# Most tiles of a decoder layer's input projection as seven-product pairs, on one pool of slots

## The chip, the cores and the metric

The kernel runs on one core of a Trainium2 chip. The metric is the device time of one execution in microseconds, the median of several runs. The engines are called by the profile's names: PE is TensorE (PEld its weight loads), DVE is VectorE, ACT is ScalarE, POOL is GpSimd, SP is SyncE, which here only issues transfers.

## The reference

One inference step of one decoder layer, float32, for a prompt of 1024 tokens and 8 samples of 4 new tokens; the kernel treats them as one matrix of T = 1056 columns.

```
h = rmsnorm(x, ln1)
aq, ak, av, sh, sB, sC, dqkv, dz, da, db, gl = split(h @ w_in)     # 1024 x 7432
oa = sliding_window_attention(aq, ak, av, sinks)                   # window 128, 8 query heads, 2 kv heads
ob = sB * causal_dwconv(sC * sh, sc_conv_w)                        # width 3
oc = gated_deltanet(silu(causal_dwconv(dqkv)), dz, da, db)         # width 4, chunked, 4 heads
merged = gate0 * (oa @ w_br_a) + gate1 * (ob @ w_br_b) + gate2 * (oc @ w_br_c)   # gates = sigmoid(gl)
x = x + merged @ w_o
gate, val = split(causal_dwconv(rmsnorm(x, ln2) @ ffn_up, ffn_conv_w))
x = x + (silu(gate) * val) @ ffn_down                              # 2816 wide
y = rmsnorm(x, ln_f)
```

The conv, attention and delta states of both groups are outputs too.

## The kernel before, in words

**Products.** Data lies with channels on the 128 partitions and the 1056 columns behind one another. Each float32 operand is split into a high part (a cast on ACT) and a low part (the rest, on POOL or DVE, `split`, L215 to L218), and each product is three: high by high, high by low, low by high. A *single tile* (`job`, `proj`, `products`, L327) is 128 output channels: three groups of 352 columns, 8 blocks of input channels, three products each, 72 in all. Its weights (512 KB) come through two buffers `wr` on SP's queue, up to three tiles ahead, and are split whole into `wh` and `wl`.

A *pair* (`class Pairs`, L1408) computes two tiles in seven block products instead of eight, in Strassen's way. The weights and h are cut into 2 by 2 blocks; the seven pieces of the weights are made in `produce`, `ahead` pieces before their use (four need a sum of 512 columns, L1365 to L1371, all a split); the seven pieces of h (`b11`, `t1`, `t2`, `b22`, `t3`, `b21`, `t4`) are built once. Each piece is 24 products of 264 columns, 168 for a pair; partial results are copied out of PSUM (L1417) or added in passing (L1195 to L1197, L1436). The pair's 1 MB of weights comes on ACT's queue; with `single` there is one pair of `wr` buffers, so that a load waits until the pair before has split its last piece, else every other pair's weights go to slots and are loaded a pair ahead.

**Stages.** The first stage multiplies h by w_in (58 tiles). ORDER fixes its jobs; capitals are pairs, `G10` being tiles 0 and 1 of the second branch's gates. Then come twelve pairs that merge the branches (`mg`), eight single tiles of w_o (`wo_job`), 22 up pairs, and the down projection, whose weight sums are formed ahead by `weight_sums` and kept in DRAM.

Four D pairs of the delta net's q, k, v use h's pieces in the first stage. The pieces lie partly in place of h's own parts: t4 overwrites the second half of `hh` and `hl` for four of eight blocks. After the last D pair `last_d` reads those halves back from `hn_d` and splits them again, since single tiles follow; for the last three pairs, G22 to G26, `h_build` makes the pieces anew from `hh + hl` (L1777, L1791, L1800).

**Background.** The elementwise and small matrix work of the branches runs as generators ("lanes", class `Lanes`). Every few products the foreground calls `bg.tick`, which lets one lane that is ready do its next step; `now` is an estimate of the time from these ticks, and waits for transfers or for other engines are estimates too. What a lane issues goes into the same engine queues as the foreground's work, in program order for PE. `bg.until` ticks, with no foreground between, until a condition holds. Lanes that need PSUM banks for a while ask `banks(n)`, of 4 (of 2 during D pairs).

The delta net is `norm_lane`, `pass1` (8 chunks of 128 tokens, three lanes), `solve` (the inverse of 32 by 32 triangles on DVE), `merge` (larger blocks of the inverse), `prep` and `scan` (the recurrence), `sample_delta` for the samples, then `out_norm`. Attention is `sample_attn`, then `attn_blocks` (loads a block of keys and queries) and three lanes `units` (two units to a block, 16 in all, the result stored behind L1644). `load_operand` builds the seven pieces of a branch's output for the merge; the merge takes the branches in the order 1, 0, 2.

**Slots.** Nearly all SBUF is two pools of 4336-byte rows: `col` with 24 slots (foreground) and `sb` with 21 (background). `room(n)` and `room2(n)` hold a lane back until n are free; `lend` and `space` let attention use part of `col`.

Of the kernel before, what the change touches and what calls it, by code (L numbers as in the profile page):

```python
# [15 lines left out]
KD = 8  # L16
# [16 lines left out]
N_COL, N_BG = 24, 21  # L33
# [88 lines left out]
class Arena:  # L122


    def __init__(self, pool, tag, n):
        self.pool, self.tag, self.n, self.live = pool, tag, n, 0
# [20 lines left out]
    def room(self, n):  # L147
        return lambda: self.live + n <= self.n
# [3 lines left out]
RESERVE = 4  # L152
# [15 lines left out]
GVWAIT = 5.0  # L168
# [4 lines left out]
def trunk(tc, A, O, cst_d):  # L173
# [17 lines left out]
    col = Arena(cp, "col", N_COL)  # L191
    sb = Arena(cp, "bg", N_BG)
# [52 lines left out]
    hn_d = [dtile(f"hn_d{m}", [128, HT]) for m in range(4)]  # L245
# [7 lines left out]
    sfcw = cp.tile([128, 836], F32, name="sfcw")  # L253
# [163 lines left out]
    hh = [col.take([128, T], F32R) for _ in range(KD)]  # L417
    hl = [col.take([128, T], F32R) for _ in range(KD)]
# [3 lines left out]
    xt = [sb.take([128, D]) for _ in range(2)] + [col.take([128, D]) for _ in range(7)]  # L422
# [29 lines left out]
    def x_group(tg):  # L452
# [32 lines left out]
        if tg == NTG - 1:  # L485
            nc.scalar.copy(ones_r, ones_f)
            nc.scalar.copy(hot[:, 46:47], ones_f[:, 0:1])
            sb.drop(7)
            col.drop(7)
# [111 lines left out]
    def sums(src, sa, r, acc, wait):  # L601


        (hi, ha), (lo, la) = grab([128, T], F32R, sb), grab([128, T], F32R, sb)
# [85 lines left out]
    def d_start(room):  # L690
        bg.until(room)
        cb, ca = grab([128, 3 + SEQ + 56], first=col)
# [3 lines left out]
    def d_end(j, cb, ca):  # L696
# [6 lines left out]
        cv, sa = grab([128, 3 + SEQ + 56], first=col)  # L703
# [10 lines left out]
    def dqkv_job(j, first=False):  # L714
        def fn(wh, wl):
            cb, ca = d_start(col.room(1))
# [54 lines left out]
    def pass1(c):  # L771

        yield lambda: done.get("qkv", 0) == 12 and done.get("ab") and sb.live + 4 <= N_BG
        kq = sb.take([128, 8, 128]).rearrange("p (h s) t -> p h s t", s=2)
        kn, bcb = pair()
        gcb, Dt = pair()
        At, qk = pair()
# [35 lines left out]
        sb.drop(4)  # L813
        bump("p1")

    def solve():

        yield lambda: done.get("p1", 0) == NB and sb.live + 4 <= N_BG
        B, X, U, tm = (sb.take([128, 32, 32]) for _ in range(4))
# [18 lines left out]
        sb.drop(4)  # L838
        bump("solve")

    def merge():


        yield lambda: done.get("p1", 0) == NB and sb.live + 7 <= N_BG
        A, Ub, W64 = ([sb.take([128, 8, 128]) for _ in range(2)] for _ in range(3))
        xw = pair2()
        X11, W = xw
        for t in W64 + A + Ub:
            nc.gpsimd.memset(t, 0.0)
        zero = W64[0].rearrange("p a b -> p (a b)")  # L850
        for b in range(2):
            dma(u_d[:, 64 * b + 32:64 * b + 64, 64 * b:64 * b + 32].rearrange("q j i -> j q i"),
                zero[0:32].rearrange("p (q i) -> p q i", i=32))
            dma(u_d[16 * b:16 * b + 16, 64:128, 0:64].rearrange("q j i -> j q i"),
                zero[0:64].rearrange("p (q i) -> p q i", i=64))
# [6 lines left out]
        yield lambda: done.get("solve") and sb.live + 5 <= N_BG  # L862
        X21, U12 = pair2()
        A64 = [sb.take([128, 8, 128]) for _ in range(2)]
        X64, U64 = sb.take([128, 16, 64]), sb.take([128, 16, 64])
# [4 lines left out]
        there = bg.arrived()  # L870
        for t in A64 + [X64, U64]:
            nc.gpsimd.memset(t, 0.0)
        for hh in range(2):
            r = slice(64 * hh, 64 * hh + 64)
            for i in range(2):
                dma(A64[i][r, :, r], a64_d[:, eight(hh, i), :])
# [1577 lines left out]
```

## Time and profile before

| | us |
|---|---|
| median of 3 runs | 1914.05 (1909.06 to 1915.11) |
| the profiled execution | 1920.69 |
| its span, first to last instruction | 1918.9 |
| PE busy | 1795.1 (94%) |
| DVE, POOL, ACT busy | 1214.4, 1044.9, 811.2 |
| first single tile's first product | 15.4 |
| D pairs | 122.7 to 222.2 |
| last gate pair ends, merge begins | 944.9 |
| merge ends, w_o begins | 1096.4 |
| up stage | 1195.7 to 1651.5 |

The times of the jobs were found by counting products on the timeline: 72 of L327 to a tile, 168 (84 in the merge) of L1408 to a pair. The page's mean duration of a matmul is longer than its share of the time, since matmuls overlap; the pace is read from stretches that hold a known number of them.

### The profile page before, as it was taken

The numbers are of one execution on the slowest core, as the hardware profiler recorded it, in microseconds if no ns is written. First come the engines' busy times: TensorE is split into PE (matmuls) and PEld (weight loads), VectorE is DVE, ScalarE is ACT, GpSimd is POOL, SyncE is SP. The second block draws the span as 40 slices with busy tenths as digits, with TensorE's granted clock in tenths as the row PEclk, the third lists the DMA queues.
The fourth block names the chain that finished last, engine by engine and source line by source line (L and its number), as shares of the span: only waits on it lengthen the run. The fifth ranks groups of instructions, "written<-read, shape, count | busy, mean of one in ns | idle before, by whom it ended". The sixth has DMA issues, their size and how long they took to land. (4 is left out here: it accounts for less than half of the span.)

```text
span 1918.9 us, 33893 instructions
## 1 busy us (share of the span) xinstructions
PE 1795.1 (94%) x12862; PEld 1753.7 (91%) x12862; DVE 1214.4 (63%) x2102; ACT 811.2 (42%) x1738; POOL 1044.9 (54%) x973
## 2 busy tenths in 40 slices
PE   6899799989999999988988899999999999899997
PEld 5798799989999998978988899999999999899996
DVE  5678755641324566686699956777777777743344
ACT  5544621112124455434554445554554544444443
POOL 3656456422334345485467745876867777334442
PEclk8999999989899999999999999999999999999998
DMA  7212597457467675944463343233232232675652
GB/s 254 87 52 85 171 325 214 129 138 210 146 201 224 207 228 162 313 166 162 156 206 99 117 140 124 72 115 110 85 111 85 94 113 80 236 243 185 186 171 89
DMA packets 298452, 301.92 MB, mean 157 GB/s; under 512 B 56549, under 2 KB 229073, under 8 KB 298273
## 3 DMA queue, kind: packets, MB, share of 16 engines
q1 hardware_dynamic: 245136, 269.34, 43.7%
q10 hardware_dynamic: 53152, 30.41, 5.5%
q8 instruction: 101, 1.65, 0.4%
q14 instruction: 63, 0.51, 0.1%
HBM read 205.33 MB, written 96.36 MB: 157 GB/s over the span
## 5 line engine op out<-in xcount | busy, mean ns | idle before, releaser
L327 PE MATMUL mm<-col,wh 128*128 128x352 f32 x2472 | 626.2, 332 | 19.5 <-ACT col L1189 9.2
L327 PEld LDWEIGHTS mm<-col,wh 128*128 128x128 f32 x2472 | 443.4, 194 | 26.2 <-ACT col L1189 9.8
L327 PE MATMUL mm<-col,wl 128*128 128x352 f32 x1248 | 413.4, 331 | 0.5 <-DVE wl L218 0.5
L327 PEld LDWEIGHTS mm<-col,wl 128*128 128x128 f32 x1248 | 241.6, 194 | 1.8 <-DVE wl L218 0.7
L218 POOL TENSOR_TENSOR wl<-wr,wh 128x1024 fp32r<-128x1024 f32 x50 | 127.9, 2559 | 191.0 <-ACT wh L217 189.1
L218 POOL TENSOR_TENSOR wl<-col,wl 128x512 fp32r<-128x512 f32 (+1 forms) x90 | 114.5, 1273 | 104.2 <-ACT wl L217 96.0
L218 POOL TENSOR_TENSOR wh<-col,wh 128x512 fp32r<-128x512 f32 (+1 forms) x82 | 101.5, 1238 | 88.0 <-ACT wh L217 68.6
L217 ACT CAST wh<-wr 128x1024 fp32r<-128x1024 f32 (+2 forms) x96 | 77.2, 810 | 126.5 <-PE mm L327 72.9
L218 DVE TENSOR_TENSOR col<-col 128x528 fp32r<-128x528 f32 x72 | 59.6, 836 | 111.3 <-ACT col L217 100.8
L1408 PE MATMUL mm<-bg,wh 128*128 128x264 f32 x762 | 116.3, 290 | 10.8 <-DVE wh L218 4.0
L1408 PE MATMUL mm<-bg,wl 128*128 128x264 f32 x744 | 114.0, 290 | 8.2 <-ACT bg L1865 4.2
L1408 PEld LDWEIGHTS mm<-bg,wh 128*128 128x128 f32 x762 | 103.0, 193 | 12.6 <-DVE wh L218 4.2
L1408 PEld LDWEIGHTS mm<-bg,wl 128*128 128x128 f32 x744 | 101.0, 193 | 9.9 <-ACT bg L1865 4.5
L1408 PE MATMUL mm<-col,wh 128*128 128x264 f32 x630 | 101.9, 289 | 5.0 <-ACT col L1417 4.0
L217 ACT CAST col<-col 128x528 fp32r<-128x528 f32 (+1 forms) x114 | 70.2, 627 | 78.0 <-POOL wh L218 31.8
L217 ACT CAST wl<-col 128x512 fp32r<-128x512 f32 (+1 forms) x104 | 59.5, 573 | 94.4 <-PE bgps L1408 32.7
L1436 DVE TENSOR_TENSOR bgps<-bgps,col 128x264 f32<-128x264 f32 x136 | 58.5, 435 | 63.2 <-PE bgps L1408 62.6
L1408 PE MATMUL mm<-col,wl 128*128 128x264 f32 x552 | 91.0, 287 | 6.0 <-DVE bgps L1436 2.5
L1408 PEld LDWEIGHTS mm<-col,wh 128*128 128x128 f32 x630 | 87.9, 192 | 6.2 <-ACT col L1417 4.5
L2171 DVE SCALAR_TENSOR_TENSOR bgps<-col,sfcw,bgps 128x358 f32<-128x358 f32 (+1 forms) x168 | 89.4, 590 | 1.1 <-ACT bgps L2169 0.3
L1408 PE MATMUL bgps<-col,wl 128*128 128x264 f32 x498 | 81.5, 293 | 3.7 <-POOL wl L218 3.3
L217 ACT CAST wh<-col 128x512 fp32r<-128x512 f32 (+1 forms) x94 | 53.0, 565 | 72.3 <-PE bgps L1408 25.6
(546 smaller groups left out, 4747.7 us busy)
## 6 DMA issues: line engine op xcount, KB each, us to landing
wr<-in_w_in SPq DMA_DIRECT2D x44, 512.0 KB
g_d<-col SPq DMA_DIRECT2D x24, 528.0 KB
ht_d<-col SPq DMA_DIRECT2D x44, 264.0 KB
col<-ht_d SPq DMA_DIRECT2D x44, 264.0 KB
bg<-in_ffn_down SPq DMA_DIRECT2D x22, 512.0 KB
wr<-in_ffn_up ACTq DMA_DIRECT2D x22, 512.0 KB
col<-in_ffn_up ACTq DMA_DIRECT2D x22, 512.0 KB
col<-g_d SPq DMA_DIRECT2D x20, 528.0 KB
```

Source lines behind the costliest of these rows:

```text
L217: nc.scalar.copy(hi, src)
L218: eng.tensor_tensor(lo, src, f32(hi), op=ALU.subtract)
L327: mm(ps[:, :TG], a[:, k, :], b[k][:, cc], start=n == 0, stop=n == last)
L1408: mm(ps, w[:, x + k, :], b[y][:, c0:c0 + HU], start=not n and piece not in NESTED, stop=n == last, skip_group_check=piece in NESTED)
L1436: nc.vector.tensor_tensor(dst, ps, x, op=ALU.add)
L2171: nc.vector.scalar_tensor_tensor(ps, cb[:, a + i:b + i], w(i), ps, op0=ALU.mult, op1=ALU.add)
```

## The change

- 19 more pairs: of the first stage's 58 tiles only d4 to d7, q0 and q1 stay single. One object `hp` runs all 26 pairs with `single` weights; for pairs from the fifth on, no low part and two instead of four sums are made on DVE, the rest on POOL. The background's limit is 2 PSUM banks in all of them.
- h's pieces are built once and stay (12 slots beside h's own 16). `last_d`, `hn_d`, the second `h_build` are gone.
- Convolution, z, k and v, q tiles get pair versions (`sc_pair`, `z_pair`, `kv_pair`, `whole_pair`). `sc_pair` multiplies in place.
- One pool of 46 slots; `kept` holds some back from the background for `own`.
- Delta net: `pass1` takes 3 slots for 4, `solve` 3 for 4; `merge` starts when `solve` is done, and loads its second half's blocks after the first half; `prep` takes 3 for 4 and starts with the scan; `sample_delta` starts beside `solve`, with two state buffers for four, and reads two of the states twice.
- Attention starts when scan and `sample_delta` are both done; blocks take 4 free slots, at most two blocks ahead; units take 2 slots for 3.
- Branch order 1, 2, 0: branch 2 waits for `out_norm`, branch 0 for attention. Branch 1's operand is built inside the last pairs.
- `weight_sums` runs in the up stage, in place, with a wait after each pass. The conv weights of the last stage get a slot at the merge.

```diff
-N_COL, N_BG = 24, 21
+N_SLOT = 46
...
-AHEADB = 3
-GAHEAD, GADD, GLO = 3, (1, 2, 3, 4), (0, 2, 4, 6)
+AHEADB = 2
...
-DPAHEAD, DPADD, DPLO, DTICK = 3, (1, 2, 3, 4), (0,), 6
+HAHEAD, HADD, HLO, DTICK, HTICK = 3, ((1, 2, 3, 4), (1, 2)), ((0,), ()), 6, 4
+KEPT = 3
...
-d4 hbd q0 d5 d6 dpairs d7 D0 D2 D8 D10 delta
-sc_start c0 h0 c1 b0 h1 c2 b1 h2 c3 b2 h3 sc_end
-v b3 k q1 q2 q3 attn_in attn sums z0 z1 z2 z3
-g10 g11 g12 g13 g14 g15 g16 g17
-g00 g01 g02 g03 g04 g05 g06 hb g07 g20 pairs g21 G22 op1 G24 G26
+d4 hb q0 d5 q1 d6 pairs d7 D0 D2 D8 D10 delta
+C0 H0 B0 C2 H2 sc_end B2
+KV Q2 attn_in attn Z0 Z2 less
+G10 G12 G14 G16 G00 G02 G04 G06 G20 G22 op1 G24 G26
...
     def solve():
-        yield lambda: done.get("p1", 0) == NB and sb.live + 4 <= N_BG
-        B, X, U, tm = (sb.take([128, 32, 32]) for _ in range(4))
+        yield lambda: done.get("p1", 0) == NB and sb.room(3)()
+        B, X, tm = (sb.take([128, 32, 32]) for _ in range(3))
+        U = B
...
     def merge():
-        yield lambda: done.get("p1", 0) == NB and sb.live + 7 <= N_BG
+        yield lambda: done.get("solve") and sb.room(6)()
...
         sb.drop(5)
-        yield
+        yield sb.room(6)
+        A64, W64 = ([sb.take([128, 8, 128]) for _ in range(2)] for _ in range(2))
+        X64, U64 = sb.take([128, 16, 64]), sb.take([128, 16, 64])
+        for t in A64 + [X64, U64] + W64:
+            nc.gpsimd.memset(t, 0.0)
...
     def sample_delta():
-        yield lambda: done.get("merge") and sb.live + 4 <= N_BG and col.live + 7 <= N_COL
+        yield lambda: done.get("p1", 0) == NB and sb.room(6)()
...
     def attn_consts():
-        yield lambda: done.get("v") and done.get("attn_in") and sb.live + 2 <= N_BG
+        yield lambda: done.get("v") and done.get("attn_in") and done.get("o", 0) == 2 and sb.room(2)()
...
-            yield lambda: done.get("satt") and done.get("o") and nb - done.get("blk", 0) < AHEADB and space() >= 7
+            yield lambda: done.get("satt") and done.get("o", 0) == 2 and nb - done.get("blk", 0) < AHEADB and sb.room(4)()
...
-            yield lambda: nb in blocks and space() >= 3
+            yield lambda: nb in blocks and sb.room(2)()
...
+    def own(shape):
+        bg.until(room2(1))
+        sb.kept -= 1
+        return sb.take(shape)
...
-            limit[0] = 2 if pp is dpp else 4
-            pp.run(i, hb, out, after)
+            limit[0] = 2
+            hp.run(i, hb, out, after)
             limit[0] = 4
...
-    order = [(b, m) for b in (1, 0, 2) for m in range(0, 8, 2)]
+    ready = {0: lambda: done.get("att", 0) == 2 * NB + 1, 2: lambda: done.get("oc", 0) == 4}
+    order = [(b, m) for b in (1, 2, 0) for m in range(0, 8, 2)]
...
     def weight_sums():
...
-            tt(s1, a21, a22, op=ALU.add)
-            tt(s2, s1, a11, op=ALU.subtract)
-            yield
+            tt(a22, a21, a22, op=ALU.add)
+            yield bg.after(SUMWAIT)
...
     def up_phase():
         ffn_start()
+        bg.add(weight_sums())
```

## Rows read from the trace of the kernel before

**Rows 1.** The page's first lines: span; engine, busy us (share of the span) xinstructions.
```profile
span 1918.9 us, 33893 instructions
...
PE 1795.1 (94%) x12862; PEld 1753.7 (91%) x12862; DVE 1214.4 (63%) x2102; ACT 811.2 (42%) x1738; POOL 1044.9 (54%) x973
```

**Rows 2.** Stretches: us, busy us of PE, PEld, DVE, ACT, POOL, PEclk, DMA, GB/s.
```profile
122.70:222.20 99.50, 88.83 (x689) 85.67 (x688) 79.68 (x87) 51.22 (x91) 59.00 (x60) 0.98 0.27 86
222.20:251.80 29.60, 21.23 (x99) 19.86 (x98) 22.95 (x16) 12.92 (x23) 15.99 (x9) 0.71 0.96 333
251.80:814.70 562.90, 547.36 (x3499) 530.82 (x3498) 269.93 (x507) 167.44 (x385) 231.65 (x176) 0.97 0.69 204
814.70:904.00 89.30, 74.56 (x472) 72.95 (x471) 72.12 (x63) 35.09 (x71) 65.20 (x33) 0.90 0.49 166
904.00:944.90 40.90, 40.90 (x339) 40.90 (x338) 23.08 (x35) 19.89 (x43) 14.34 (x12) 1.00 0.32 113
944.90:1096.40 151.50, 131.59 (x977) 126.71 (x976) 143.45 (x264) 75.73 (x199) 104.74 (x96) 0.94 0.46 155
1223.10:1651.50 428.40, 428.40 (x3530) 427.82 (x3528) 325.87 (x694) 214.26 (x500) 308.12 (x384) 1.00 0.29 94
```

**Rows 3.** Stretches, PE only: length, busy us (xproducts), granted clock, DMA share, GB/s.
```profile
358.90:404.90 46.00, 46.00 (x291) 1.00 0.32 89
231.20:248.30 17.10, 12.74 (x45) 0.50 0.96 368
```

**Rows 4.** Timeline of PE: start, us, line, tiles, [idle before <- releaser].
```profile
231.86 1.34 PE L1408 MATMUL mm<-bg,wl 128*128 128x264 f32 x4 [4.18 <-ACT bg L1865]
...
868.33 0.96 PE L327 MATMUL mm<-col,wh 128*128 128x352 f32 x2 [8.33 <-ACT col L1189]
```

**Rows 5.** Groups, 122.7 to 222.2: count, busy us, mean ns, idle before.
```profile
L218 POOL TENSOR_TENSOR wh<-bg,wh 128x512 fp32r<-128x512 f32 x8 | 14.8, 1846 | 3.7 <-ACT wh L217 2.3 <-issue 1.3
...
L613 PE MATMUL bgps<-bg,hot 128*48 128x352 f32 x36 | 7.9, 328 | 5.0 <-DVE bg L218 3.2 <-ACT bg L217 1.8
...
L217 ACT CAST wh<-bg 128x512 fp32r<-128x512 f32 x8 | 5.0, 622 | 15.7 <-DVE bg L1371 6.5 <-DVE bg L1365 5.6 <-DVE bg L1369 1.5
```

**Rows 6.** Timeline around the load of the second D pair's weights.
```profile
142.86 0.38 ACTq L182 DMA_DIRECT2D wr<-in_w_in  x1
...
147.25 0.70 DVE L1365 TENSOR_TENSOR bg<-wr 128x512 f32<-128x512 f32 x1 [1.89 <-DMA wr<-in_w_in]
```

**Rows 7.** Groups of POOL, 251.8 to 404.9.
```profile
L218 POOL TENSOR_TENSOR wl<-wr,wh 128x1024 fp32r<-128x1024 f32 x12 | 29.2, 2430 | 23.8 <-ACT wh L217 23.8
```

**Rows 8.** The same stretch, POOL only: length, busy us, granted clock, DMA share, GB/s.
```profile
251.80:404.90 153.10, 75.85 (x66) 1.00 0.66 189
```

**Rows 9.** Groups of POOL, 222.2 to 944.9.
```profile
L218 POOL TENSOR_TENSOR wl<-wr,wh 128x1024 fp32r<-128x1024 f32 x38 | 97.2, 2558 | 153.5 <-ACT wh L217 151.6 <-PE mm L327 1.8
...
L1777 POOL TENSOR_TENSOR bg<-col 128x1056 f32<-128x1056 f32 x4 | 14.4, 3592 | 0.0
```

**Rows 10.** Waits of PE, 404.9 to 581.8: us in total, times, longest.
```profile
PE bgps L885 <- DMA bg<-xu_d: 6.3, 1, 6.3
```

**Rows 11.** Single lines: count, ns min/median/max, first to last start.
```profile
L796 PE MATMUL bgps<-bg x64: 377/379/381, 287.9 to 346.6; 128*128 128x256 f32 x64
...
L932 ACT COPY bg<-bgps x2: 585/586/586, 445.6 to 447.4; 128x512 f32<-128x512 f32 x2
...
L1014 ACT COPY bg<-bgps x3: 585/585/591, 513.1 to 550.5; 128x512 f32<-128x512 f32 x3
...
L1673 POOL COPY bg<-bg x2: 283/288/292, 521.6 to 524.5; 64x128 f32<-64x128 f32 x2
...
L1732 ACT COPY bg<-bgps x16: 163/167/169, 576.1 to 578.8; 64x16 f32<-64x16 f32 x16
...
L1644 DVE TENSOR_TENSOR col<-bgps,col x7: 669/681/683, 619.7 to 845.5; 64x512 f32<-64x512 f32 x7
```

**Rows 12.** Groups of POOL, 1223.1 to 1651.5.
```profile
L218 POOL TENSOR_TENSOR wl<-col,wl 128x512 fp32r<-128x512 f32 x41 | 54.7, 1334 | 38.9 <-ACT wl L217 37.1 <-PE bgps L1408 1.8
```

More of the change, by code (lines that the diff above doesn't have):

```diff
@@ L869, in merge @@
                 dma(Ub[i][r, :, r], xu_d[1][2 * b + 1, eight(hh, i)].rearrange("q i j -> i q j"))
[L870 to L876, printed above, removed]
-        for b, hh, r, gs in four:
-            d = slice(64 * hh + 32 * b, 64 * hh + 32 * b + 32), slice(32 * b, 32 * b + 32)
-            dma(X64[d[0], :, d[1]], xu_d[0][b, gs].rearrange("q i j -> i q j"))
-            dma(U64[d[0], :, d[1]], xu_d[1][2 + b, gs].rearrange("q i j -> i q j"))
-        yield there
+        yield bg.arrived()
         yield banks(1)
@@ L948, in prep @@
         for c in range(NB):
-            yield lambda: done.get("merge") and len(pre) < 2 and sb.live + 4 <= N_BG
+            yield lambda: done.get("scan") and len(pre) < 2 and sb.room(3)()
             kn, vT = pair()
             qT, ebc = pair()
-            qk, ke = pair()
-            vb, U = pair()
+            qk, U = pair()
+            ke, vb = vT, ebc
             dma(kn, qkv_d[c][:, 4:8, :])
@@ L1251, in sc_job, with times @@
-    def sc_job(kind, t):
-        c0, fn = {"c": (C_SC, sc_c), "h": (C_SH, sc_h), "b": (C_SB, sc_b)}[kind]
-        job(w_cols(w_in, c0 + t * 128), KD, fn(t))
-    named["sc_start"], named["sc_end"] = lambda: step(sc_start), lambda: step(sc_end)
-    for t in range(4):
-        for kind in "chb":
-            named[f"{kind}{t}"] = lambda kind=kind, t=t: sc_job(kind, t)
+    def times(dst, ps, x, part, view=lambda ap: ap):
+        y = ps[:, part]
+        if x is not None:
+            y = x[:, part]
+            nc.vector.tensor_tensor(y, ps[:, part], y, op=ALU.add)
+        nc.vector.tensor_tensor(dst, dst, view(y), op=ALU.mult)
@@ L1437, in summed, with stored, whole_pair, out @@
         return dst
[L1440 to L1451 removed]
+    def stored(dst_d, evac_of):
         def fn(wh, wl):
[L1453 to L1454 removed]
+            bg.until(room2(1))
+            t, ta = grab([128, T])
             proj(wh, wl, hh, hl, KD, evac_of(t))
[L1456 to L1462 removed]
+            dma(dst_d, t)
+            ta.drop()
+        return fn
+    def whole_pair(then, func=AF.Copy, scale=1.0):
+        ts = []
+        for _ in range(2):
+            ts.append(own([128, T]))
+        def out(which, c0, ps, x, more):
+            d = ts[which][:, c0:c0 + HU]
+            if x is None:
+                nc.scalar.activation(d, ps, func, scale=scale)
+            else:
+                nc.vector.tensor_tensor(d, ps, x, op=ALU.add)
+        def finish(which):
+            t = ts[which]
+            if func != AF.Copy or scale != 1.0:
+                cc = slice(which * HT, T)
+                nc.scalar.activation(t[:, cc], t[:, cc], func, scale=scale)
+            then(which, t)
+        return out, finish
     def token_major(src, blks, out):
@@ L1636, in units @@
             n, last = 0, 2 * len(kbs) - 1
-            for kb in kbs:
-                for b in (PTh, PTl):
-                    mm(ps, (vz if kb else vp)[:, kv, :], b[:, kb, :], start=n == 0, stop=n == last)
+            for kb, t in zip(kbs, pt):
+                for b in range(2):
+                    mm(ps, (vz if kb else vp)[:, kv, :], t[:, b, :], start=n == 0, stop=n == last)
                     n += 1
@@ L1886, in fn @@
                 last_sums()
-                for j in range(2, pp.ahead):
-                    pp.produce(j)
-                if not pp.single:
-                    pp.load(1)
-            end = i + 1 == len(pp.srcs)
+                for j in range(2, hp.ahead):
+                    hp.produce(j)
+            end = i + 1 == len(hp.srcs)
             out, finish = start()
+            hp.tick = DTICK if i < 4 else HTICK
             def after(j, piece):
@@ L2051, in weight_sums @@
         for p in range(NPAIR):
-            yield sb.room(3)
-            wa, wb, s = (sb.take([128, 1024]) for _ in range(3))
+            yield room2(4)
+            wa, wb = (sb.take([128, 1024]) for _ in range(2))
             for i, w in enumerate((wa, wb)):
```

493 lines of the change are left out of this document (228 added, 265 removed).

## The prediction

> **What bounds the kernel now.** I read the page's first part, then a table of stretches, then the waits of those in which TensorE is not full. TensorE is busy 1795.1 of 1918.9 us [rows 1]; columns removed from it count where it is full, elsewhere the wait counts. The table [rows 2] cuts out four pairs (122.7 to 222.2), one tile, c0 (to 251.8), 34 tiles beside delta net and attention (to 814.7), four tiles and the first gate pair (to 904.0), two gate pairs (to 944.9, TensorE full), the merge (to 1096.4), and 21 of the 22 up pairs from 1223.1, full throughout. Units: four undisturbed tiles take 46.0 us [rows 3], 11.50 each (72 products of 352 columns); 21 pairs take 428.4 [rows 2], 20.40 each (168 of 264 columns). A pair replaces two tiles, so it gives 23.00 - 20.40 = 2.60 us.
>
> A wait costs more than its gap: from 231.2, around the 4.18 us gap that ends at 231.9 [rows 4], the granted clock is 0.50 for 17.1 us [rows 3], the lower of its two levels (1.2 of 2.4 GHz).
>
> **The change part by part**, against the profiled execution's own 1920.69 us (1918.9 of span, 1.8 around it).
>
> *a. Nineteen more pairs.* 38 of the 44 single tiles of w_in become pairs: 12 gated-convolution tiles, v and k, two q, four z, 18 gate tiles. 19 x 2.60 = 49.4 us, all on TensorE's path. That q1 moves ahead of D0 changes no sum.
>
> *b. The restoring and rebuilding of h's pieces go.* Before, D10 ends with h's lost half read back and split again, and c0 waits: 29.6 us and 99 products [rows 2], 72 of its own (11.5 us) and 27 others (some 3 at full clock). Some 15 are lost; the norm lane that also works there stays, so I take 12. The second build (L1777, 14.4 us on GpSimd alone [rows 9]) lies in 814.7 to 904.0: 89.3 us for four tiles (46.0) and a pair (20.4) leave 22.9, of which some 3 are attention's products; its longest wait is 8.33 us [rows 4]. I take 20. Together -32. What is late next there is attention, no longer beside the rebuild.
>
> *c. New waits in the pairs.* Each pair adds seven casts (ScalarE, 0.62 each [rows 5]), seven low parts and four sums of 512 on GpSimd or VectorE, and seven evacuations per half. Its weights come into one buffer, loaded when the pair before has split its last piece. Upper end: the four D pairs work so already, 99.5 us [rows 2] less 4 x 20.4 and less 36 norm-sum products [rows 5] of 0.16 us (5.8): 12 lost, 3.0 a pair. Lower end: the two last gate pairs lose nothing (40.9 for two). So 0 to 66 for 22 pairs. The D pairs are the dearest: VectorE is busy 79.7 of 99.5 there with the four-tap convolutions, and 269.9 of 562.9 in 251.8 to 814.7. The load is not their loss: issued at 142.86, it is read at 147.25 [rows 6], 2 us before the next pair begins. I take 1.0 a pair, nearer the gate pairs: +22.
> GpSimd is what could be late first. In 251.8 to 404.9 it is busy 75.9 [rows 8], of which 29.2 are tile splits [rows 7]; the other 46.7, beside 7.5 pairs of 9 x 1.33 us [rows 12], make 136 of 153 us, and at the D pairs' 1.85 a piece [rows 5] 172: late by up to 19, inside the range of c. Over 222 to 945 it has 327 us (the sum of its column in rows 2); less splits 97 [rows 9], sums some 59 and the rebuild some 28, plus 22 x 12, it stays near 410 of some 670.
>
> *d. Delta net on fewer slots.* Its inverse (the merge lane) now starts after solve and sample step, in two halves that clear and load one after the other. Its products stand in TensorE's queue among the foreground's; one already waited 6.3 us for a transfer [rows 10]. Two more such transfers: 0 to +20. I take +6: the PSUM limit of 2 lets fewer such products queue early.
>
> *e. Attention later, branch order 1, 2, 0.* Before [rows 11], pass 1's last product starts at 346.6, the inverse ends at 448, sample attention runs from 521.6 (its loads some 12 earlier) to 579, and the units' results come from 619.7 to 845.5, 15.05 apart. After, with a start some 10 later (q1 in front): pass 1 to 357; the sample step, which lay behind the inverse, some 70 plus two reloads of 10, to 447; the inverse, 50 from solve's end by the timeline plus some 25 in series, to 522; a first chunk of 22 and seven at 18.7 (the three from 513.1 to 550.5, where no unit ran) to 675; attention now waits for both delta results: sample attention 69 to 744, first result 41 later, fifteen more to 1011, its operand some 15 more, an estimate (14 casts of 0.62 alone are 8.7). The first stage ends at 944.9 - 49.4 - 32 + 22 + 6 = 891.5; the last four merge pairs, which alone need that operand, begin two thirds of 151.5 [rows 2] later, at 993. So some 33 late at the old pace, or 40 early at 10 us a unit, without weight sums and scan beside it. The other cost: VectorE, busy 143.5 of 151.5 in the merge, gets attention's last units. -10 to +40; I take +9, nearer the faster pace, since for two thirds of its old run attention shared the ticks with both.
>
> *f. Weight sums move to the up stage.* 44 passes of 1.33 us on GpSimd (59), which is busy 308.1 of 428.4 there [rows 2]: 86%, with the pieces made four ahead (4 x 20.4/7 = 11.7 us). That covers it; if its 11 passes a pair stretched by 0.5 as in the D pairs, 115 more, GpSimd would be over. 0 to +20; I take +3. The sums' 23 MB move into a DMA share of 0.29.
>
> Sum: -49.4 - 32 + 22 + 6 + 9 + 3 = -41.4, so 1879.3 for this execution, which lies 6.6 above the median of the three runs (1914.05): **1873 us**.
>
> **Weighed against the skill.** Behind D10 the DMA share is 0.96 at 333 GB/s [rows 2]. The Trainium skill (DMA: Bandwidth & Descriptors, Issuing engines are not separate DMA queues) says that transfers interleave on the same 16 engines whichever engine issues them. By it the pairs' queue on ScalarE buys no bandwidth, and their half load of 4.4 us would take about twice that there, an estimate; the sum would be 4 us higher in each of the first two or three pairs, about 1883. No run here shows it for pairs: the D pairs loaded at a share of 0.27.
>
> **Rivals.**
> 1. *The pairs' waits eat the gain.* Every pair behaves as a D pair: c becomes +66, the sum +2.6, the time 1917; at 2.3 a pair 1902. For: single-buffer weights, GpSimd near full behind D10. Against: 5.0 of the D pairs' 10.7 us of idle are norm sums waiting for VectorE and ScalarE [rows 5], which later pairs lack.
> 2. *Slower: attention comes too late for the last four merge pairs.* The mechanism is the pool: behind delta net some 11 slots serve blocks, units and out-norm, where before some 13 to 15 did, and pairs let the background hold 2 PSUM banks instead of 4, one of them out-norm's. TensorE stands still in the ninth merge pair until the operand is there. At 22 us a unit the last result is at 785 + 15 x 22 = 1115, the operand at 1130, 137 behind 993: 1873 - 9 + 137 = 2001. It decides from a lateness of 50 (the gain of 41 and the 9 of e), an operand at 1043, some 16 us a unit. For: at 15.05 a unit VectorE was only half busy, so slots or lanes set the pace. Against: a unit takes two slots instead of three, a block four instead of seven, and the lanes beside it are fewer.
> 3. *Larger gain.* Pairs run as the gate pairs (c at 6), attention in time (e at 0): 1848; with the merge freer by 10, 1838.
> 4. *GpSimd bounds the up stage.* f at +20: 1890, seen as gaps there, where there were none.
> 5. *Something of h is rebuilt after all*: the diff leaves no rebuild; b is then lost: 1905.
>
> **How the numbers follow.** Forecast with its own range 1845 to 1900: 50%. Rival 1 (1900 to 1922): 16%. Rival 2 (from 1915 up): 15%. Rival 3 (under 1845): 12%. Rival 4: 5%. Rival 5: 2%. Within 0.3%, about what a measurement of this kernel can tell from no change, is 1908.3 to 1919.8. Faster: 50 + 12 + 5 + 2 and six of rival 1 = 75%; same: eight, of rival 1 and the edge of 2; slower: 17%. The range leaves out the far part of rivals 2 and 3: 1832 to 1930.
>
> **What would show it.** a: pairs of 20.4 to 21.4 us from 235 to 890. b: no additions of hh and hl of 1056; no 4 us gap behind D10. c: TensorE's gaps in the pairs, by GpSimd's low parts behind D10. d: the inverse's products waiting for transfers. e: the last attention result between 930 and 1010 and no gap over 10 us in the ninth merge pair. f: up pairs still at 20.4 with GpSimd at 86%. The prediction is wrong if the merge stands still for attention, or if pairs average over 23 us.

## The result and the profile after

The changed kernel takes 1944.39 us (median of 4 runs, 1937.47 to 1947.02), the kernel before beside it 1914.58: a ratio of 1.0151, 95% interval 1.0113 to 1.0189. It is slower by 30 us, where 41 less were forecast. The profiled execution took 1947.02 us; all stretches below are of profiled executions.

First lines of the page of the changed kernel, to be read beside [rows 1]:

```profile
span 1945.2 us, 35371 instructions
...
PE 1776.9 (91%) x13318; PEld 1725.1 (89%) x13318; DVE 1259.8 (65%) x2219; ACT 860.2 (44%) x1883; POOL 1182.6 (61%) x1111
```

TensorE works 18.2 us less than before and the span is 26.3 us longer, so 44.5 us more are waits. The stretches that answer to [rows 2], in the same columns: D pairs, the six pairs C0 to B2, ten pairs beside delta net (KV to G16 with the end of the scan), the eight last gate pairs beside attention, the merge, and 21 up pairs:

```profile
147.50:242.10 94.60, 89.36 (x711) 86.68 (x710) 78.21 (x86) 50.74 (x90) 59.58 (x57) 1.00 0.31 99
242.10:437.80 195.70, 159.81 (x1093) 152.92 (x1092) 123.16 (x214) 49.89 (x108) 137.94 (x119) 0.89 0.64 181
437.80:690.30 252.50, 248.01 (x1912) 242.11 (x1912) 92.41 (x205) 80.07 (x157) 126.57 (x106) 0.93 0.59 168
690.30:945.00 254.70, 225.85 (x1708) 216.07 (x1707) 162.56 (x266) 137.11 (x355) 125.08 (x94) 0.95 0.54 160
945.00:1124.40 179.40, 148.33 (x1027) 138.75 (x1026) 173.16 (x312) 92.95 (x241) 120.29 (x103) 0.91 0.38 135
1252.00:1682.90 430.90, 429.12 (x3530) 427.84 (x3528) 335.65 (x694) 214.94 (x501) 366.66 (x434) 1.00 0.43 143
```

| us, profiled executions | before | changed | difference |
|---|---|---|---|
| start to D0's first product | 122.7 | 147.5 | +24.8 (13.5 of it q1, moved here) |
| D pairs | 99.5 | 94.6 | -4.9 |
| rest of the first stage | 722.7 | 702.9 | -19.8 (q1 moved out) |
| merge | 151.5 | 179.4 | +27.9 |
| w_o, up stage, rest | 822.5 | 820.8 | -1.7 |

The first stage ends where it ended before, at 945, instead of 891.5 as forecast, and the merge is longer. In C0 to G26, 702.9 us, 448 are the 22 pairs at 20.36 and some 131 other products; 124 are neither, that is, waits and time at the lower clock. Before, that remainder was some 66 of 723, beside some 147 of other products.

Single lines of the changed kernel, as in [rows 11]: first pass, scan, end of attention's sample step, results of attention's 16 units (count, ns min/median/max, first to last start):

```profile
L792 PE MATMUL bgps<-slot x64: 377/379/763, 308.0 to 397.0; 128*128 128x256 f32 x64
...
L1011 ACT COPY slot<-bgps x8: 586/587/587, 575.4 to 693.4; 128x512 f32<-128x512 f32 x8
...
L1750 ACT COPY slot<-bgps x16: 163/166/169, 730.5 to 733.2; 64x16 f32<-64x16 f32 x16
...
L1663 DVE TENSOR_TENSOR slot<-bgps,slot x16: 670/674/683, 771.4 to 1002.4; 64x512 f32<-64x512 f32 x16
```

Attention's units keep their pace (231 us for 15 intervals, 15.4 each; before 225.8), but begin 152 us later and end 157 later, at 1002 instead of 845: 57 us into the merge. Of the three operands of the merge, the first is loaded from 885 to 913 and its pieces are cast until 968 (before: until 943, with the merge beginning at 945); the other two are loaded from 959 to 1026 and cast until 1064.

### The profile page after: what moved, and what is told of

Its sections match the earlier page's. It is cut to its first block, busy times and chain, and to the rows that moved or that the text cites. A ratio compares the mean times of both kernels' runs of the same rounds, so it can differ in the third digit from the quotient of the medians.

```text
span 1945.2 us, 35371 instructions
## 1 busy us (share of the span) xinstructions
PE 1776.9 (91%) x13318; PEld 1725.1 (89%) x13318; DVE 1259.8 (65%) x2219; ACT 860.2 (44%) x1883; POOL 1182.6 (61%) x1111
## 4 chain that ended last, share of the span: by engine, by line
PE 54%; DVE 16%; DMA 11%; issue 5%; POOL 5%; ACT 5%; SPq 2%; ACTq 0%; DVEq 0%; POOLq 0%
PE mm L1417 17%; PE bgps L1417 13%; PE mm L323 7%; DMA wr<-in_w_in 3%; SPq L181 2%; DVE slot L356 2%; PE bgps L2308 2%; PE bgps L2309 2%; PE bgps L2310 2%; PE mm L2309 1%; PE mm L2310 1%; PE mm L2308 1%; POOL wh L216 1%; DVE slot L1303 1%; ACT slot L1625 1%
## 5 line engine op out<-in xcount | busy, mean ns | idle before, releaser
L1417 PE MATMUL mm<-slot,wh 128*128 128x264 f32 x2256 | 328.8, 295 | 32.7 <-ACT slot L1426 8.8
L1417 PE MATMUL mm<-slot,wl 128*128 128x264 f32 x2256 | 322.2, 291 | 21.4 <-DVE slot L1210 6.1
L1417 PEld LDWEIGHTS mm<-slot,wh 128*128 128x128 f32 x2256 | 301.7, 196 | 40.7 <-ACT slot L1426 10.7
L1417 PEld LDWEIGHTS mm<-slot,wl 128*128 128x128 f32 x2256 | 295.0, 192 | 30.4 <-DVE slot L1210 5.6
L216 POOL TENSOR_TENSOR wl<-slot,wl 128x512 fp32r<-128x512 f32 (+1 forms) x142 | 191.6, 1349 | 137.8 <-ACT wl L215 123.4
L216 POOL TENSOR_TENSOR wh<-slot,wh 128x512 fp32r<-128x512 f32 (+1 forms) x133 | 182.1, 1369 | 139.5 <-ACT wh L215 134.6
L1417 PE MATMUL bgps<-slot,wl 128*128 128x264 f32 x1680 | 247.3, 298 | 7.9 <-POOL wl L216 3.4
L1417 PE MATMUL bgps<-slot,wh 128*128 128x264 f32 x1680 | 242.7, 296 | 12.6 <-DVE slot L1968 5.7
L1417 PEld LDWEIGHTS bgps<-slot,wl 128*128 128x128 f32 x1680 | 228.0, 199 | 12.8 <-POOL wl L216 4.2
L1417 PEld LDWEIGHTS bgps<-slot,wh 128*128 128x128 f32 x1680 | 226.2, 199 | 14.6 <-DVE slot L1968 5.8
L215 ACT CAST wh<-slot 128x512 fp32r<-128x512 f32 (+1 forms) x145 | 84.6, 585 | 162.0 <-POOL slot L1378 41.2
L323 PEld LDWEIGHTS mm<-slot,wh 128*128 128x128 f32 x672 | 119.7, 192 | 10.9 <-DVE slot L718 6.5
```

The lines of the kernel that those rows point to most:

```text
L215: nc.scalar.copy(hi, src)
L216: eng.tensor_tensor(lo, src, f32(hi), op=ALU.subtract)
L323: mm(ps[:, :TG], a[:, k, :], b[k][:, cc], start=n == 0, stop=n == last)
L1417: mm(ps, w[:, x + k, :], b[y][:, c0:c0 + HU], start=not n and piece not in NESTED, stop=n == last, skip_group_check=piece in NESTED)
```

## Experiments

**Delta net and attention left out of both kernels, then attention alone.** Edit in each (zeros are written for what is left out):

```
-        for i in range(3): bg.add(seq(*[pass1(c) for c in range(i, NB, 3)]))
-        bg.add(solve()) ... bg.add(seq(sample_delta(), out_norm()))
+        bg.add(no_delta())          # e1, e2 only
-    bg_later = lambda: (bg.add(attn_consts()), bg.add(sample_attn()), bg.add(attn_end()))
+    bg_later = lambda: bg.add(no_attn())
```

> The changed kernel without delta net (first pass, inverse, scan, sample step, output norm) and without attention: zeros are written in their place. Norm lane, convolutions, gates, merge and all later stages stay. Theory A (the pairs are as fast as forecast, and what took the gain is the background work that stands in TensorE's queue and on the helper engines beside them): the 14 pairs from C0 to G16 lasted 448 us for 285 of own work and the eight gate pairs behind them 255 for 163; nearly all of the excess goes but some 20 us behind D10, where the norm lane stays, and the merge goes back to some 150: about 1690 to 1710 us. Theory B (the pairs themselves are slow: casts, low parts, sums, evacuations and the one weight buffer): only the background's products (about 110 us) and the merge's 28 go: about 1790 to 1810, with pairs still at 23 us or more.

> The same left out of the kernel before. Its first stage holds some 147 us of products that are not its tiles' own, nearly all of them the background's, and some 20 us of waits beside the two builds of h's pieces, which stay: about 1740 to 1760 us. Theory A: the changed kernel without background is 45 to 65 us faster than this one (49 for the pairs, some 30 for the builds, less 11 for the start and some for the norm lane). Theory B: it is no faster than this one, or slower.

> The changed kernel with delta net, but without attention (its result is zeros). Theory A1 (attention, which now runs from 680 to 1004 us, slows the gate pairs by its chains and the merge by its tail): the gate pairs from 690 on fall from 31.8 to some 21 to 22 us each and the merge from 179 to about 150: about 1825 to 1840 us. Rival A2 (delta net behind D10 did most of the damage, attention costs only its products, some 50 us, and the merge stays slow): about 1890 us.

> The same left out of the kernel before. There attention ran beside single tiles, whose weights are split two tiles ahead: its products (some 50 us) and about 10 us of waits go: about 1850 to 1860 us. Theory A1: the changed kernel without attention is then 15 to 30 us faster than this one; rival A2: it is some 30 us slower, as much as the whole kernel is.

| median us | before | changed | changed less before |
|---|---|---|---|
| neither delta net nor attention | 1733.73 | 1698.04 | -35.7 |
| delta net only | 1850.81 | 1835.31 | -15.5 |
| both | 1914.0 | 1944.4 | +30.4 |

(Ratios to the kernel before: e1 0.8874, 0.8853 to 0.8895; e2 0.9054, 0.9033 to 0.9076; e3 0.959, 0.9565 to 0.9615; e4 0.9663, 0.9638 to 0.9687.) e1, e3 and e4 lie in the ranges of theories A and A1, e2 6 us below its own; the first pair's difference, 36 us, is 9 short of theory A's, the second's within A1's. Stretches of the changed kernel without background, C0 to B0 and eleven pairs from Z2 on:

```profile
241.60:332.40 90.80, 71.50 (x510) 68.66 (x509) 49.14 (x62) 24.42 (x52) 64.68 (x53) 0.91 0.71 234
458.70:683.10 224.40, 224.40 (x1850) 224.40 (x1849) 46.74 (x92) 93.92 (x188) 130.53 (x99) 1.00 0.35 116
```

The changed kernel without attention, the last eight gate pairs and the merge:

```profile
691.40:864.80 173.40, 171.28 (x1393) 169.34 (x1392) 81.14 (x104) 78.05 (x156) 117.08 (x80) 1.00 0.53 183
864.80:1013.50 148.70, 127.54 (x977) 122.90 (x976) 143.04 (x264) 75.02 (x200) 106.30 (x97) 0.97 0.45 158
```

TensorE is busy for 224.40 of 224.40 us: left alone, a pair takes 20.40 with one weight buffer and all its casts. Only C0 to B0 lose some 30 us without the background; the norm lane and the convolutions are still beside them. TensorE's three longest waits in that stretch (us in total, times, longest; 241.6 to 332.4) are for GpSimd's low parts and for ScalarE:

```profile
PE bgps L1425 <- POOL wl L216: 6.5, 3, 3.0
PE mm L1425 <- ACT wh L215: 3.5, 1, 3.5
PE mm L1425 <- POOL wh L216: 3.0, 2, 1.9
```

Without attention the eight gate pairs take 173.4 instead of 254.7 and the merge 148.7 instead of 179.4. So delta net costs 137 us in the changed kernel and 117 before, attention 109 and 63. These differences, 20 and 46 us, are the turn from -36 to +30. Theory B (the pairs themselves are slow) and rival A2 (delta net did most of the damage) fall.

**What makes attention dearer: its start, the banks, the look-ahead, VectorE in the merge?** Four edits of the changed kernel:

```
-        yield lambda: ... done.get("o", 0) == 2 ...     # e5: attn_consts, attn_blocks
+        yield lambda: ... done.get("o", 0) ...          #     and merge order (1, 0, 2)
-            limit[0] = 2                                # e6
+            limit[0] = 2 if i < 4 else 4
-HAHEAD ... = 3        hp = Pairs(8, [], HAHEAD, 4, ...  # e7, two slots for pieces 5 and 6
+HAHEAD ... = 4        hp = Pairs(8, [], HAHEAD, 6, ...
-MAHEAD, MADD, MLO = 4, (1, 2), (0, 2, 4, 6)             # e8
+MAHEAD, MADD, MLO = 4, (1, 2), (0, 4)
```

> The changed kernel in full, but attention waits for the sample step of delta net alone, no longer for the scan as well, and the merge takes its branches in the order 1, 0, 2 as before. Theory A1 (attention is late: it starts at 680 and its last units lie in the merge): it starts by some 520, beside the scan, its last result comes before 900, the merge falls from 179 to about 150 us, and the gates' waits change little: 1905 to 1920 us. Rival S (slots: beside the scan's six or seven there is no room for the sample step of attention's seven, so it starts no earlier, or the scan becomes late instead): 1940 us or more.

> The changed kernel in full, but from the fifth pair on the background may hold four PSUM banks instead of two. Theory P (the limit of two makes delta net and attention wait for a bank before each step, so that their chains are long and late): attention's 16 units take less than their 240 us, the merge loses less to its tail: 1910 to 1930 us. Rival Q (banks are not scarce; the wait is TensorE's queue in order behind VectorE's and ScalarE's parts of the chains): within 6 us of 1944, or slower, because pairs now wait for banks that the background holds.

> The changed kernel in full, but the seven pieces of a pair are made four ahead instead of three, in six buffers instead of four; the two buffers are two slots that delta net and attention then lack. Theory L (the single tiles were split two tiles ahead, some 23 us, the pieces only three ahead, 8.7 us, so each delay of a helper engine now reaches TensorE): the 59 us lost from C0 to B2 fall to some 35 and those beside attention by some 15: 1905 to 1920 us. Rival Q (TensorE waits in order for the background's own chains, and the pieces are not what is late): 1938 to 1950; with fewer slots for attention, slower still.

> The changed kernel in full, but in the merge two of the four low parts that VectorE makes in a pair (24 of 48 in all, some 0.75 us each) go to GpSimd. Theory V (VectorE bounds the merge since attention's tail lies in it: busy 173 of 179 us): the merge falls by 10 to 18 us, 1926 to 1934. Rival W (the merge waits for chains, not for VectorE's time; GpSimd's low parts take longer and stretch VectorE's): within 5 us of 1944.

Measured: e5 1935.78 us (ratio 1.0106, 1.0068 to 1.0144), e6 1946.34 (1.0171, 1.014 to 1.0202), e7 1961.92 (1.0248, 1.0214 to 1.0282), e8 1946.12 (1.0162, 1.0136 to 1.0188). None came near its main expectation. What they do to the two parts of the time is worth more than the totals (counted on the timelines of the profiled executions, with two runs told below; the time is the median):

| | first stage ends | last result of attention | merge ends | time |
|---|---|---|---|---|
| before | 944.9 | 845 | 1096.4 | 1914.1 |
| changed | 945.0 | 1002 | 1124.4 | 1944.4 |
| e5 attention earlier | 902.4 | 954 (output norm 1020) | 1106.5 | 1935.8 |
| e6 four banks | 930.3 | 1009 | 1123.3 | 1946.3 |
| e7 pieces four ahead | 901.9 | 1045 | 1134.0 | 1961.9 |
| e9 delta net behind B2 | 872.0 | 1092 | 1170.6 | 1994.6 |
| e10 two slots less | 918.5 | 1040 | 1137.7 | 1957.9 |

The first stage can end 15 to 73 us sooner, and the kernel gains 9 us at best, which is not clear of noise (the intervals of e5 and of the changed kernel overlap): the merge takes back what the tiles gave. In these runs the time goes with the last result of the background, not with the tiles. e8 says that it is not VectorE's time either, which falls from 173.2 of 179.4 us to

```profile
945.70:1124.60 178.90, 147.03 (x1032) 138.24 (x1031) 160.82 (x288) 93.20 (x242) 137.46 (x126) 0.91 0.38 133
```

with the same length. e5 shows where the chain is tight. Attention beside the scan starts 150 us sooner (771 to 621), but the scan's eight chunks then take 296 us instead of 118, and attention's units 22 instead of 15.4:

```profile
L1011 ACT COPY slot<-bgps x8: 566/587/588, 607.0 to 902.8; 128x512 f32<-128x512 f32 x8
...
L1663 DVE TENSOR_TENSOR slot<-bgps,slot x16: 674/683/685, 621.3 to 953.9; 64x512 f32<-64x512 f32 x16
```

e7 did in part what it was made for: C0 falls from 36.9 to 24.8 us, H0 from 28.6 to 22.8, B2 from 34.3 to 22.3, but B0 stays (37.4 and 36.3) and C2 and H2 take 3 to 4 us more; in all C0 to B2 fall from 195.7 to 171.5. Look-ahead was short there, by the first part of theory L. But attention's end moved back by 42 us, most likely by the two slots that e7 took from the background (e10 below takes two and changes nothing else). Its units' results:

```profile
L1665 DVE TENSOR_TENSOR slot<-bgps,slot x16: 649/674/684, 788.2 to 1044.5; 64x512 f32<-64x512 f32 x16
```

Stretches of the same run, C0 to B2, KV (TensorE waits once for 17.5 us for VectorE, which is busy 35.1 of 41.2, 30.7 of it with delta net's inverse, L824 and L826) and the merge:

```profile
247.40:418.90 171.50, 149.76 (x1078) 144.72 (x1077) 112.17 (x188) 46.55 (x100) 132.24 (x110) 0.92 0.64 187
418.90:460.10 41.20, 23.02 (x171) 22.60 (x170) 35.12 (x66) 7.51 (x16) 16.69 (x13) 0.79 0.50 122
901.90:1134.00 232.10, 175.74 (x1140) 162.70 (x1138) 214.33 (x386) 119.13 (x320) 128.55 (x109) 0.86 0.38 123
```

My first theory, that the pairs' waits are the loss, falls with this. The second: **the chain of the background (first pass, inverse, scan, attention, operands) has become the bound, and the number of free slots sets its pace.** h's pieces hold 12 slots to the end of the stage, with 3 of scratch, 16 of h and 2 of constants 33 of 46; 13 are left, 3 of them kept for the tiles. Before, some 27 of 45 were free until the second build.

**The chain later, the slots fewer.** Edits of the changed kernel:

```
-d4 ... D10 delta / C0 H0 B0 C2 H2 sc_end B2 / KV ...      # e9
+d4 ... D10 / C0 H0 B0 C2 H2 sc_end B2 / delta KV ...
     def less():                                           # e10, undone when the merge begins
-        sb.kept -= 1
+        sb.kept += 1
```

> The changed kernel in full, but delta net is started behind the pair B2 instead of behind D10. Theory C (what is bound is the chain of the background, delta net, then attention, then the operands, from 242 to 1004 us, and not the tiles): C0 to B2 fall from 196 to some 154 us as without background, but the chain starts some 150 us later, and the end moves by 100 to 150: 2040 to 2090 us. Rival D (the tiles are the bound, and delta net's first pass behind D10 is what made them slow): C0 to B2 give 40 us and most of it stays: 1905 to 1925.

> The changed kernel in full, but from the last z pair to the merge the background may use two slots fewer. Theory S (slots set the pace of attention, 15 us a unit with some nine or ten slots): its last result comes 30 to 60 us later than 1004, and the end moves by 20 to 50: 1965 to 1995 us. Rival (the waits in its own chains, or TensorE's queue, set the pace): within 8 us of 1944.

e9: 1994.58 us (ratio 1.0425, 1.04 to 1.045); C0 to B2 take 151 us, as theory C said, the first stage ends 73 us sooner, and the kernel is 50 us slower. The rise is half of what C gave. Delta net started 151 us later, but took 391 us from its start to its scan's end instead of 451; attention's last result came 89 us later and the merge's end 46, so the end does not follow the chain one to one. e10: 1957.87 (1.0233, 1.0209 to 1.0256), 13.5 us slower, below theory S's 20 and outside the rival's 8, so neither was right on the time; the last result comes 37 us later, as S had it:

```profile
L1663 DVE TENSOR_TENSOR slot<-bgps,slot x16: 671/682/683, 768.3 to 1039.9; 64x512 f32<-64x512 f32 x16
```

**The same loss made in the kernel before, without one pair more.** Eight slots of its background pool are taken from the tile v to the second build:

```
+    def hold():
+        for _ in range(8):
+            bg.until(lambda: sb.live < sb.n)
+            sb.take([128, SLOT])
-c0 ... h3 sc_end / v b3 ...  g05 g06 hb g07
+c0 ... h3 sc_end hold / v b3 ...  g05 g06 free hb g07
```

> The kernel before, but from the tile v to the second build of h's pieces eight slots are taken and left unused, so that the background has about as few as in the changed kernel; all tiles stay single. Theory S (the missing slots, not the pairs beside it, put attention off): scan and attention no longer run side by side, attention's last result moves from 847 to 930 or later, and the time to 1955 to 2000 us. Rival P (the pairs put it off: their pieces, two PSUM banks, their waits): the last result stays before 880 and the time within 15 us of 1914.

1968.72 us, ratio 1.0283 (1.0263 to 1.0303): 53 us slower, by theory S. The results of attention (11 of 16 have this form) and the scan:

```profile
L1651 DVE TENSOR_TENSOR col<-bgps,col x11: 671/675/684, 714.1 to 986.9; 64x512 f32<-64x512 f32 x11
...
L1014 ACT COPY bg<-bgps x8: 586/587/590, 474.9 to 643.3; 128x512 f32<-128x512 f32 x8
```

The merge's first two pairs, 91.8 us with TensorE busy for 49.9 at a granted clock of 0.70 (before they took 23.8):

```profile
926.10:1017.90 91.80, 49.91 (x276) 44.70 (x277) 78.35 (x133) 49.08 (x132) 30.96 (x23) 0.70 0.36 116
```

With few slots the scan ends sooner (643 instead of 678), attention's first result comes at 714 instead of 620 and its last at 987. The units come 18.2 us apart. The first stage even ends 19 us sooner (926.1); the whole loss lies in the merge, whose first operand is loaded from 921 to 931 and cast until 990, when attention has ended. That is the changed kernel's picture, made by slots alone. How large it is in the changed kernel this run does not say: here a block still asks for seven slots and a unit for three, there for four and two. No run gave the changed kernel slots back.

**The D pairs, in either kernel; the weight sums alone.** e11 and e12 edit the kernel before, e14 the changed one, e15 is e11 with e12, e16 adds two gate pairs:

```
-d4 hbd q0 d5 d6 dpairs d7 D0 D2 D8 D10 delta                  # e11, e15, e16
+d4 q0 d5 hdrop d6 d7 d0 d1 d2 d3 d8 d9 d10 d11 delta          # hdrop: frees h's 8 slots
-v b3 ... attn_in attn sums z0 ...                             # e12, e15, e16
+v b3 ... attn_in attn z0 ...      # weight_sums() is added when the up stage begins
-d4 hb q0 d5 q1 d6 pairs d7 D0 D2 D8 D10 delta                 # e14
+d4 q0 d5 q1 d6 d7 d0 d1 d2 d3 d8 d9 d10 hb d11 pairs delta
-g05 g06 hb g07 g20 pairs g21 G22 ...                          # e16
+hb g05 pairs G06 G20 G22 ...
```

> The kernel before, but the eight tiles of D0 to D10 go as single tiles: no pieces of h are built for them, and none of h is restored behind D10. Theory R (step b: the restoring costs 12 us or more, and the D pairs lose more than their 10 us of products): from d0 to the end of c0 some 110 us instead of 129: 1890 to 1902 us. Rival N (c0 waits for the norm lane and the convolutions, which stay): 1908 to 1918, no gain beyond the waits in the D pairs.

> The kernel before with step f alone: the weight sums of the down stage run in the up stage, in two slots instead of three. Forecast of step f: the up stage pays 0 to 5 us; the first stage loses 59 us of GpSimd and three slots' use, where GpSimd's rebuild made gaps of 8 and 5 us: 1902 to 1914 us. Rival (the sums cost the up stage 20 us, GpSimd over its time there): 1925 to 1935.

> The changed kernel, but the eight tiles of D0 to D10 go as single tiles, and h's pieces are built while d11 runs, so that C0 is the first pair. Theory R (building the pieces beside d4 to d7 and the D pairs is what they cost): d5 loses its 12 us of waits, the chain of the background starts 20 to 30 us earlier, and the end moves by as much: 1910 to 1925 us. Rival (the build then collides with the norm lane and C0 to B0, and attention is bound by slots anyway): 1940 us or more.

> The kernel before with single D tiles and with the weight sums in the up stage, both. The two gave 29 and 10 us alone and lie in different stretches: 1873 to 1882 us if they add; if the first stage's end is set by attention's chain in both, 1880 to 1886.

> As the run before it, and h's pieces are built behind g04 instead of g06, so that G06 and G20 go as pairs as well. Two pairs more are worth 5.2 us of products: 1868 to 1878 us; if the build now stands beside attention's last units and each waits for the other, 1880 to 1890.

e11: **1885.05 us, ratio 0.9848 (0.9822 to 0.9875), faster than both kernels**, and more than theory R gave. The eight D tiles, c0, and d5 of that run:

```profile
112.90:211.90 99.00, 98.69 (x614) 96.59 (x613) 70.39 (x71) 35.27 (x40) 29.23 (x42) 1.00 0.37 123
211.90:228.30 16.40, 13.55 (x76) 13.22 (x76) 8.73 (x6) 5.48 (x11) 12.60 (x8) 0.90 0.97 305
75.10:88.80 13.70, 13.11 (x84) 12.62 (x83) 4.16 (x8) 6.83 (x10) 2.40 (x1) 1.00 0.34 118
```

Eight single tiles take 99.0 us, four D pairs took 99.5 [rows 2]: the pairs' 10 us of products were eaten by waits (and the last 21 products of D10 lie behind those 99.5 us). c0 takes 16.4 instead of 29.6, d5 13.7 instead of 21.3 since no pieces are built beside it.

e12: 1903.88 (0.9949, 0.9931 to 0.9967). The first stage ends 23 us sooner and attention at 805 instead of 845; the up stage's 21 pairs pay 9 us (428.4 to 437.5). e14: 1941.13 (1.0137, 1.0113 to 1.0161), no gain. C0 begins 14 us sooner, but the build of the pieces now lies between d11 and C0, beside the norm lane, and C0 stops for

```profile
256.50 1.25 PE L1417 MATMUL bgps<-slot,wl 128*128 128x264 f32 x4 [25.06 <-ACT wl L215]
```

(timeline of TensorE: start, us, tiles, idle time before it and what ended it), while attention's last result comes at 1006 as ever. e15: 1885.22 (0.9839, 0.9814 to 0.9863): the two parts don't add. The number is in the second case of its expectation, but not for that reason: the first stage does end 13 us sooner than in e11, and the up stage pays 8. e16: 1892.48 (0.9893, 0.9872 to 0.9914). There TensorE stands 19 us in G06 waiting for the build, which had one tile of cover instead of three; so it says nothing on attention's last units.

## Why the prediction was wrong

**a, right.** A pair takes 20.40 where nothing disturbs it (e1). The gain of 49 us on TensorE's products is there.

**b, wrong in kind.** I took 12 us for the restoring and 20 for the second build. The restoring's wait did go, but the same place waits for something else: C0 to B0 lose 30 us without any background (e1), where c0 lost some 12 (e2: 27.0 us, less 11.5 and 3). For the kernel before, 12 was about right: with nothing restored, c0 falls from 29.6 to 16.4 (e11). The second build costs nothing where attention is out of the way: in e2 and e4 each tile from g06 to g21 takes 11.5 us. So the gap of 8.33 us there [rows 4] needs attention, and the build by itself is hidden. The stretch c0 of e2 and the four tiles of e4:

```profile
222.80:249.80 27.00, 18.50 (x99) 17.11 (x98) 20.58 (x15) 12.54 (x22) 15.22 (x10) 0.87 0.93 335
...
767.70:813.60 45.90, 45.90 (x290) 45.90 (x289) 5.63 (x7) 12.19 (x22) 12.24 (x7) 1.00 0.38 129
```

And I left out that the pieces are still built beside d4 to d7: d5 takes 27.6 us instead of 21.3, and the first product comes at 19.7 instead of 15.4; together 11 us that stood in no term.

**c and d, the step that failed by most.** 28 us were forecast for waits in the pairs and for the inverse. The remainder of 66 us before was to fall by b's 32; it rose to 124, so some 90 against 28 (16 us less of other products offset a part). A pair took 26.0 us without the other products, (448 + 124)/22, over the 23 that I had named as a sign of being wrong. My lower end, the two last gate pairs, is right without background from C2 on; my upper end, the D pairs, was no upper end, and it was read too low: 21 of their 672 products run behind 222.2 [rows 2], so they lost 3.7 us a pair and not 3.0. I took the pairs' own work for the cause of waits, and most of it is the work beside them: some 30 us of the remainder, C0 to B0, stay without the background. Behind D10 the waits of TensorE come from every helper (us in total, times, longest; 242.1 to 437.8):

```profile
PE mm L1417 <- DVE slot L1210: 6.1, 2, 5.4
PE bgps L1417 <- ACT wh L215: 4.8, 1, 4.8
PE bgps L792 <- issue: 4.3, 1, 4.3
PE mm L1417 <- ACT wh L215: 3.5, 2, 2.6
PE mm L1417 <- ACT slot L1426: 3.5, 2, 2.9
PE bgps L1417 <- POOL wl L216: 3.4, 2, 1.8
```

GpSimd, which I held to be late first, is busy 138 of 196 us and stands behind VectorE and ScalarE in that list. That does not clear it: without the background its low parts are the largest wait of TensorE in C0 to B0 (e1 above, 9.5 us), and in the stretch of this list ScalarE's casts of weight pieces waited 21 us for the sums that GpSimd makes (L1378, L1380). The clock was granted at 0.89 there, so that the gaps cost again as [rows 3] showed. C0's weights were late too: the second half's load was issued at 236.58 and read at 245.67, 9.1 us at a DMA share of 0.89 (236 to 246), where a D pair's took 4.4 [rows 6]:

```profile
236.58 0.37 ACTq L181 DMA_DIRECT2D wr<-in_w_in  x1
...
245.67 1.68 DVE L1374 TENSOR_TENSOR slot<-wr 128x512 f32<-128x512 f32 x1 [5.87 <-DMA wr<-in_w_in]
```

The Trainium skill (DMA: Bandwidth & Descriptors, Issuing engines are not separate DMA queues) says that the transfers of all issuing engines interleave on the same 16 DMA engines, by which about twice the 4.4 us was estimated; this one load agrees.

**e, the second step that failed.** The last result was forecast at 1011 and measured at 1002, but that is luck: pass 1's last product came at 397 instead of 357, the scan's last result at 693 instead of 675, and attention's sample step then took 40 us instead of 69. Only the pace of the units, 15.4 us against 15.05, was right. I took 9 us, because I leaned to 10 us a unit, and because I held the last operand to be the only one that attention holds up. Units take two slots instead of three, but have half as many slots to take them from. And attention's tail stands in the way of the first operand: its four loads, each of which waits for three free slots, go out from 885 to 913, where without attention they take from 800.8 to 802.7 (e3), and its pieces are cast until 968, 23 us into the merge (e3: until 858, 7 us ahead of it). In the first merge pair, 29.3 us instead of 11.4, TensorE works through attention's products and waits for these pieces (L1293, L1294; timeline, 963 to 969):

```profile
964.74 0.81 PE L1417 MATMUL mm<-slot,wh 128*128 128x264 f32 x2 [3.65 <-ACT slot L1293]
967.25 2.05 PE L1417 MATMUL mm<-slot,wh 128*128 128x264 f32 x7 [1.70 <-POOL slot L1294]
```

So the merge is late from its first pairs on, not at the ninth: the four pairs of the first operand take 70.4 us (945 to 1015) instead of 47.4, the other eight 109.0 instead of 104.1. Of the 23 us more in the four, TensorE is busy for some 15 (attention's products, and a clock granted at 0.88 to 0.96 in the first three) and idle for 8. That the loads were late for want of slots, and not for another wait of their chain, is argued from e3 and e13, not shown. In the gate pairs, which no term of e held, attention costs 81 us more (254.7 against 173.4 without it); TensorE is busy for 55 of them.

**f, right:** from 428.4 to 430.9 us for 21 up pairs, with GpSimd busy 366.7; in the kernel before the same step cost 9 (e12), inside the range of 0 to 20. What it gives in the first stage was not in the sum: 23 us in the kernel before (e12).

**Rivals.** The second, attention too late, is what happened, but at the old pace and at another place, in the gate pairs and the first merge pairs; that its mechanism (the pool) is behind it rests on e10 and e13. My point of decision, an operand at 1043, was worked out with the merge beginning at 891. The first rival's sum (+2.6) was closer than the forecast, but its cause, each pair behaving as a D pair, is refuted by e1. e9 shows that less slack in the chain costs, e10 and e13 that fewer slots make it later; what each of the 13 slots is worth was not measured.

## What to carry to other kernels

Where two chains run side by side, price a change by what it does to the other chain's resources: e13 took eight buffers away and changed nothing else, and 53 us went. A saving on the busy engine is worth little once the other chain ends last: in the table of e5 to e10 the first stage ended up to 73 us sooner, and no run was clearly faster than the changed kernel. Leave the background out of both kernels first: that one pair of runs split +30 into -36 and +66.

## What the runs showed of the hardware

VectorE's additions with both inputs in SBUF often take longer when GpSimd works beside them, those with one input in PSUM did not. The same line in the short-convolution pairs of the changed kernel (count, ns min/median/max, first to last start):

```profile
L1211 DVE TENSOR_TENSOR slot<-slot x30: 178/436/1547, 297.8 to 427.6; 128x264 f32<-128x264 f32 x14, 128x232 f32<-128x232 f32 x8, 128x32 f32<-128x32 f32 x8
L1211 DVE TENSOR_TENSOR slot<-slot,mm x8: 417/418/430, 310.9 to 431.5; 128x264 f32<-128x264 f32 x8
```

Of those with 264 elements the longest took 1547 ns with two SBUF inputs and 430 with one; five of the eight with one had GpSimd busy beside them throughout. Over all float32 additions and subtractions of 528 columns up to the merge's end, 12 with GpSimd beside them for less than 0.05 us took 0.70 us each and 24 with more 1.21 on average, 2.84 at most. The Trainium skill (SBUF — State Buffer, Who interferes with whom) states that the port pair which the two engines share is an exclusive lock, that a VectorE instruction with two SBUF inputs contends with a GpSimd instruction that reads SBUF, and that one with at most one SBUF input, outside two-port modes, does not; these rows agree. How much of the difference this makes was not measured: VectorE's busy time up to the up stage is 749.6 us before and 776.1 after, with 117 more instructions in it.
